# Earlier squares, a shorter look-ahead, later attention constants and a closing norm in fewer steps, in a two-layer encoder trunk

## The chip, the core and the metric

The kernel runs on one core of one Trainium2 chip. The metric is device time in microseconds (us) of one execution. A core has five engines with instruction streams of their own: TensorE (PE in the profile; its weight loads are PEld), VectorE (DVE), ScalarE (ACT), GpSimd (POOL) and SyncE (SP), which here only issues DMA transfers. They wait for one another through semaphores.

## The reference, cut to what matters

256 tokens, width 1024, two layers, all in float32:

```
for l in range(2):
    x = x + 1/2 * SwiGLU_1(RMSNorm(x))        # 1024 -> 2816 gate, up; -> 1024
    h = RMSNorm(x)
    q, k, v (A and B) = h @ w_in[l]
    oA = windowed attention with a sink logit per head
    oB = softmax1 - lambda * softmax2, per-head RMSNorm * (1 - lambda_init)
    x = x + concat(oA, oB) @ w_out[l]
    x = x + 1/2 * SwiGLU_2(RMSNorm(x))
return RMSNorm(x)
# RMSNorm(x) = x / sqrt(mean(x*x) + eps) * g
# SwiGLU(h)  = (silu(h @ w_gate) * (h @ w_up)) @ w_down
# lambda = exp(sum(q1*k1)) - exp(sum(q2*k2)) + lambda_init
```

## The kernel before, in words

**Products.** Every float32 product is made of three products in a faster format (fp32r): an operand is split in a high part, a cast, and a low part, the operand less its high part. PE then adds high x high, low x high and high x low. For weights the cast is ScalarE's and the subtraction VectorE's: `CAST w<-raw` and `TENSOR_TENSOR w<-raw,w` in the profile, 440 of each. Activations are split in the same way (`CAST s<-ps`, then `TENSOR_TENSOR s<-ps,s`).

**Weights.** The program walks through one list of weight steps (`Step`, line 92). A step is a raw tile of 1 MB, of which six can be held (`N_RAW`), and two half-steps, each of which is split into a high and a low tile from a pool of 28 (`s4`). `emit_dma` (147) puts the load on SP's queue, `emit_split` (175) writes the cast and the subtraction into the program. `ahead(n)` (212) writes all splits up to half-step n; `weights()` (233) calls it with twice the step in use plus `look[0]`, and a `Split` calls it again between its halves. So `look[0]` says by how many half-steps the splits stand ahead of PE's products in the program: 8 in an FFN (`IN_FFN`), 6 elsewhere (`IN_MIX`).

**FFN** (`ffn`, 566). The 2816 hidden columns go in five groups of 512 and a piece of 256. Group 0 and 1 are plain: four steps of gate and up weights, `silu` on ScalarE, `hidden` (h = up * silu(gate) on VectorE), then `turn`, which transposes h on PE and splits it, and `down`, the products with w_down. Groups 2, 3 and 4 (`SEVEN`) go through `by_seven` (598): the 2x2 block product with seven products in place of eight. For it, sums of weight blocks are needed: two of a group's raw tiles get a second block added by an accumulating transfer that GpSimd issues (`gather`, 125), and further sums are VectorE's (`plus`, 130, `TENSOR_TENSOR raw<-raw,raw`). Sums of the activations are made once, in group 1 (`make_sums`, 333: the q and v tiles). `down` of a group stands inside the next group. After the last piece, `ffn_end` (704) does the last groups' products: `group(0)`, with `turn` of the last piece in it, and `tail`, the products of the last piece.

**Order.** `Kept` (41) keeps the program's order on each engine, so the order of calls in the source is the order on PE, ScalarE and VectorE. All their instructions carry line 50, that of the helper; they are told apart by their tiles. An engine that waits holds everything behind it.

**The places around the change.** At the start (`take_x`, 410) x arrives in four pieces, is transposed and multiplied by the norm's gain (`pair`, 302), and the first weights are split; then the four squares with their sums (`squares`, 298: ACTIVATE junk<-xk with a read of the accumulator), the norm's factors (`stats`, 368) and small transfers and operations on GpSimd (`constants`, 452). A silu on ScalarE needs the factors, and PE gets no PSUM bank for the next products until the first silu has read one. `attention_constants` (475) makes distances, lambda and gains for the attention: a PE transpose, eleven VectorE operations, an exp on ScalarE. It is handed to the first FFN as `aside` and called in group 1, line 691; the same place in the last FFN calls `final_gain` (974), which loads the final norm's gain (512 KB, on SP). At the end, `close` (993) adds the last products to x and squares the result on ScalarE, and `finish` (1002) reduces the sums on VectorE, takes the power -1/2 on GpSimd, multiplies half the columns on ScalarE and half on VectorE, and issues two outputs on SP.

Of the kernel before, what the change touches and what calls it, by code (L numbers as in the profile page):

```python
# [9 lines left out]
F32 = mybir.dt.float32  # L10
F32R = mybir.dt.float32r
AF = mybir.ActivationFunctionType
ALU = mybir.AluOpType

P = 128
D = 1024
# [7 lines left out]
EPS = 1e-6  # L24
# [5 lines left out]
IN_FFN, IN_MIX = 8, 6  # L30
# [4 lines left out]
def trunk(ctx: ExitStack, tc: tile.TileContext, x, n1, g1, u1, d1, nm, w_in, sink,  # L35
          lq1, lk1, lq2, lk2, subln, w_out, n2, g2, u2, d2, nf, out):
    nc = tc.nc
    sp = nc.sync
# [18 lines left out]
    pe, act, dve, pool = Kept(nc.tensor), Kept(nc.scalar), Kept(nc.vector), Kept(nc.gpsimd)  # L57

    const = ctx.enter_context(tc.tile_pool(name="const", bufs=1))
# [20 lines left out]
    def tmp(tag="tmp", bufs=5, shape=(P, 2, 256), dt=F32):  # L80
        return tp.tile(list(shape), dt, tag=tag, bufs=bufs, name=nm_(tag))
# [127 lines left out]
    look = [IN_MIX]  # L209
# [190 lines left out]
    mhalf = const.tile([P, 8], F32, name="mhalf")  # L400
# [9 lines left out]
    def take_x(k):  # L410

        g, u = early
        if k == 0:
            for j in (0, 1):
                sl = norm.turn(j)
                next(g)
                norm.operands(j, sl)
                next(u)
        elif k == 1:
            for e in (g, u, g, u):  # L420
                next(e)
            norm.pair(2)
            ahead(5)
            norm.pair(3)
        elif k == 2:
            ahead(7)
            for t in range(2):
                for h in range(2):
                    norm.squares(t, h * 512, 512)
            norm.stats()  # L430
            constants()

# [133 lines left out]
    def ffn(norm, aside=None, before=None, final=False):  # L566
        def silu(out_, acc, t):
            act.activation(out_, acc, AF.Silu, scale=norm.r[:, t:t + 1])
            return out_

        def gate(gs):
            g = []
            for t in range(2):
                n = gs[t].shape[1]
                g.append(silu(tmp().rearrange("p a n -> p (a n)")[:, :n], gs[t], t))
            return g

        def up(h, acc, g, t):
            n = acc.shape[1]
            dve.scalar_tensor_tensor(h[:, t, :n], in0=acc, scalar=norm.hr[:, t:t + 1], in1=g, op0=ALU.mult, op1=ALU.mult)  # L580

        def hidden(g, us):
            h = blk(F32)
            for t in range(2):
                up(h, us[t], g[t], t)
            return h

        def prod(xo, w):
            acc = bank()
            for k in range(4):  # L590
                hi, lo = w.part(k)
                xh, xl = xo(k)
                pe.matmul(acc, lhsT=xh, rhs=hi, start=k == 0, stop=False)
                pe.matmul(acc, lhsT=xl, rhs=hi, start=False, stop=False)
                pe.matmul(acc, lhsT=xh, rhs=lo, start=False, stop=k == 3)
            return acc

        def by_seven(h, g):


            flat = lambda: tmp().rearrange("p a n -> p (a n)")

            def put(o, x, y, op):
                dve.tensor_tensor(o, x, y, op=op)
                return o

            m1, m7 = flat(), flat()
            act.copy(m1, prod(norm.quarter(0, 0), weights()))
            act.copy(m7, prod(norm.summed(2), weights(held=True)))
            hT = turn(h, 2)  # L610
            p2 = prod(norm.quarter(0, 1), weights())
            g0 = put(flat(), p2, m1, ALU.add)
            p3 = prod(norm.summed(3), weights())
            silu(g0, g0, 0)
            down(hT, g - 1, 0, weights())
            h = blk(F32)
            p5 = prod(norm.summed(0), weights())
            late = g == max(SEVEN)
            p6 = prod(norm.summed(1), weights(look[0] - 5 if late else 0, late))
            u2 = put(flat(), p6, m1, ALU.subtract)  # L620
            u3 = put(m7, m7, u2, ALU.add)
            p4 = prod(norm.quarter(1, 1), weights(look[0] - 4 if late else 0, late))
            g1 = put(m1, p4, u3, ALU.subtract)
            w = weights(look[0] - 3 if late else 0)
            silu(g1, g1, 1)
            put(u3, u3, p5, ALU.subtract)
            put(u2, u2, p5, ALU.subtract)
            put(u2, u2, p3, ALU.add)
            up(h, u2, g0, 0)
            up(h, u3, g1, 1)  # L630
            down(hT, g - 1, 1, w)
            return h

        def turn(hs, n):
            out_ = []
            for i in range(n):
                sl = halves(bank())
                for c in range(2):
                    for t in range(2):
                        pe.transpose(sl[:, c, t * P:(t + 1) * P], hs[:, t, (2 * i + c) * P:(2 * i + c + 1) * P], ident)  # L640
                hb = blk()
                split(hb, sl)
                out_.append(hb)
            return out_

        accs = [[bank(), bank()] for _ in range(2)]

        def down(hT, g, h, w):
            tokens(accs[h], [None] * (2 * g) + hT, w, 4 * g, last=(FC - 1, G4 - 1) if final and h else FC - 1)


        gs, us = [bank(), bank()], [bank(), bank()]
        if before is None:
            before = norm.late
        look[0] = IN_FFN
        before(0)
        ws = (weights(), weights(2))
        for k in (0, 2):
            if k:
                before(1)  # L660
            for sl, w in zip((gs, us), ws):
                tokens(sl, norm.xs, w, 0, (k, k + 1))
        before(2)
        tokens(gs, norm.xs, weights(), 4)
        g = gate(gs)
        tokens(us, norm.xs, weights(), 4)
        h = hidden(g, us)
        for n in range(1, NGRP):
            sums = norm.make_sums() if n + 1 == min(SEVEN, default=0) else iter(())
            if n in SEVEN:  # L670
                look[0] = IN_FFN - max(0, n - 2)
                h = by_seven(h, n)
                continue
            gs = [bank(), bank()]
            tokens(gs, norm.xs, weights(), 0)
            hT = turn(h, 2)
            norm.copies()
            tokens(gs, norm.xs, weights(), 4)
            g = gate(gs)
            next(sums, None)  # L680
            us = [bank(), bank()]
            for k0 in (0, 4):
                tokens(us, norm.xs, weights(), k0)
                next(sums, None)
            h = hidden(g, us)
            for hh in range(2):
                down(hT, n - 1, hh, weights())
                if hh == 0:
                    next(sums, None)
                    if aside is not None:  # L690
                        aside()
                        aside = None

        gu = [bank(), bank()]
        tokens(gu, norm.xs, weights(), 0)
        hT = turn(h, 2)
        tokens(gu, norm.xs, weights(), 4)
        h = hidden(gate([b[:, 0:256] for b in gu]), [b[:, 256:512] for b in gu])
        return accs, hT, lambda: turn(h, 1)

    BY_TOKENS = [(k, t) for t in range(2) for k in range(2)]
# [266 lines left out]
            res.add(1, t)  # L968
        nxt_norm.late = res.late

    fss = const.tile([P, 2, 4], F32, name="fss")
    gf = []

    def final_gain():
        gf.append(blk(F32))
        sp.dma_start(gf[0].rearrange("p a n -> p (a n)"), nf.partition_broadcast(P))
        pool.memset(fss, 0.0)


    for l in range(DEPTH):  # L980
# [9 lines left out]
            ffn_close(parts, norm)  # L990


    def close(t, c0, n, acc):

        xv = xk[:, t, c0:c0 + n]
        dve.tensor_tensor(xv, acc, xv, op=ALU.add)
        jk = tmp().rearrange("p a n -> p (a n)")
        act.activation(jk[:, :n], xv, AF.Square, accum_out=fss[:, t, c0 // 256:c0 // 256 + 1])
        if c0 == 0:
            pool.tensor_tensor(xv, xv, gf[0][:, 0], op=ALU.mult)  # L1000

    def finish(t):
        rf = tmp("rf", 2, (P, 1))
        dve.tensor_reduce(rf, fss[:, t], axis=mybir.AxisListType.X, op=ALU.add)
        dve.tensor_scalar(rf, rf, 1.0 / D, EPS, op0=ALU.mult, op1=ALU.add)
        pool.tensor_tensor(rf, rf, mhalf[:, 0:1], op=ALU.pow)
        ob = blk(F32)
        act.mul(ob[:, 0], xk[:, t, 0:512], rf)
        dve.scalar_tensor_tensor(ob[:, 1], in0=xk[:, t, 512:D], scalar=rf, in1=gf[0][:, 1], op0=ALU.mult, op1=ALU.mult)
        for j in range(2):  # L1010
            sp.dma_start(out[0, t * P:(t + 1) * P, j * 512:(j + 1) * 512], ob[:, j])

    accs = parts[0]
    group, tail = ffn_end(parts, ((FC - 1), FC - 1))
# [46 lines left out]
```

## Time and profile before

| what | value |
|---|---|
| three timed runs | median 940.94 us (940.77 to 941.16) |
| the profiled execution | 938.1 us, its span 936.3 us |
| mean granted TensorE clock | 0.997 |
| PE busy | 922.1 us, 98% of the span, 4796 matmuls |
| VectorE busy | 757.3 us, 81%, 1066 instructions |
| ScalarE busy | 573.2 us, 61%, 901 instructions |
| GpSimd busy | 51.3 us, 5% |
| chain that ended last | PE 92%, DMA 4%, DVE 1%, ACT 1% |
| mean DMA rate | 208 GB/s, 194.58 MB |

How to read it: times are us from the start of the span. A line of the timeline has a start, a duration (for several instructions in a row, first start to last end), the engine, the line, the operation, output tile <- input tiles, the shapes, and how many; in brackets the idle time ahead of it and what ended it. A line of the waits has the waiting engine and tile, what it waited for, the total in us, how often, and the longest. A line of the windows has, for one stretch, its length and each engine's busy time and count of instructions; PEclk is the granted TensorE clock as a share of full speed. SPq, ACTq and POOLq are an engine's issue of transfers.

### The profile page before, as it was taken

To read this page: it belongs to the slowest core of one execution; us is meant where nothing else is said; L and a number is where in the kernel's file an instruction comes from. 1 tells how busy PE (TensorE), PEld (TensorE's weight loads), DVE (VectorE), ACT (ScalarE), POOL (GpSimd) and SP (SyncE) were. 2 spreads that over 40 slices of the span, in tenths; PEclk is the share of its full clock that TensorE was granted. 3 is DMA by queue.
4 is the path that set the end of the run, shared out by engine and by line. 5 is a ranking of instruction groups with operands and counts; after the bars stand their busy time and mean duration, and the time that the engine had idled before them with its cause. 6 is when DMAs were issued, how large, how long until landed. Compare 5 with 4: busy or idle time off the path is not lost.

```text
span 936.3 us, 12676 instructions
## 1 busy us (share of the span) xinstructions
PE 922.1 (98%) x4796; PEld 782.2 (84%) x4796; DVE 757.3 (81%) x1066; ACT 573.2 (61%) x901; POOL 51.3 (5%) x73
## 2 busy tenths in 40 slices
PE   8999999999999999999999999999999999999997
PEld 6788778899898888888888888888999888888886
DVE  6679999859866588999866799996697566799992
ACT  6847675548745666576475565665577476466562
POOL 0400100000000000100001000000000001001001
PEclk9999999999999999999999999999999999999999
DMA  9986897928425857797667597887462467697821
GB/s 336 355 219 159 247 289 249 270 91 225 136 91 180 249 156 225 206 288 256 240 227 221 135 288 202 240 284 217 150 193 91 135 205 202 166 299 204 249 91 46
DMA packets 110893, 194.58 MB, mean 208 GB/s; under 512 B 3566, under 2 KB 31280, under 8 KB 110832
## 3 DMA queue, kind: packets, MB, share of 16 engines
q1 hardware_dynamic: 96816, 167.27, 53.3%
q0 software_dynamic: 12928, 25.46, 15.4%
q10 hardware_dynamic: 1088, 1.05, 0.3%
q8 instruction: 37, 0.61, 0.3%
q14 instruction: 24, 0.20, 0.1%
HBM read 192.71 MB, written 1.05 MB: 207 GB/s over the span
## 4 chain that ended last, share of the span: by engine, by line
PE 92%; DMA 4%; DVE 1%; ACT 1%; issue 1%; SPq 0%; ACTq 0%; POOLq 0%; POOL 0%; DVEq 0%
PE ps L50 92%; DMA raw<-in_ffn_w_up_dram 2%; DMA raw<-in_ffn_w_gate_dram 2%; DVE w L50 1%; DMA xk<-in_x_dram 1%; ACT w L50 0%; DVE tmp L50 0%; ACT junk L50 0%; DVE s L50 0%; ACT tmp L50 0%; SPq L152 0%; ACT L50 0%; ACTq L50 0%; DVE xk L50 0%; POOLq L1056 0%
## 5 line engine op out<-in xcount | busy, mean ns | idle before, releaser
L50 PE MATMUL ps<-w,s 128*128 128x512 f32 (+1 forms) x2754 | 642.1, 391 | 2.1 <-ACT tmp L50 2.1
L50 PEld LDWEIGHTS ps<-w,s 128*128 128x128 f32 x2754 | 512.7, 189 | 107.8 <-ACT tmp L50 2.6
L50 DVE TENSOR_TENSOR w<-raw,w 128x1024 fp32r<-128x1024 f32 (+1 forms) x440 | 460.8, 1093 | 57.0 <-ACT w L50 55.8
L50 ACT CAST w<-raw 128x1024 fp32r<-128x1024 f32 (+1 forms) x440 | 391.1, 948 | 85.8 <-DVE raw L50 71.0
L50 PE MATMUL ps<-w,q 128*128 128x512 f32 x432 | 101.9, 389 | 0.0
L50 PEld LDWEIGHTS ps<-w,q 128*128 128x128 f32 x432 | 81.1, 188 | 16.8
L50 PE MATMUL ps<-s,w 128*128 128x256 f32 x672 | 84.1, 285 | 0.0
L50 PEld LDWEIGHTS ps<-s,w 128*128 128x128 f32 x672 | 81.7, 192 | 1.1
L50 ACT ACTIVATE s<-ps,gcol 128x256 fp32r<-128x256 f32 (+1 forms) x80 | 31.5, 488 | 48.0 <-PE ps L50 48.0
L50 ACT CAST s<-ps 128x512 fp32r<-128x512 f32 x48 | 26.1, 593 | 51.9 <-PE ps L50 51.9
L50 DVE TENSOR_TENSOR raw<-raw,raw 128x1024 f32<-128x1024 f32 x48 | 56.4, 1216 | 0.0
L50 DVE TENSOR_TENSOR s<-ps,s 128x512 fp32r<-128x512 f32 x48 | 31.0, 684 | 27.1 <-ACT s L50 27.1
L50 POOL DMA_DIRECT2D raw<-in_ffn_w_up_dram x24 | 31.0, 1293 | 354.9 <-DVE w L50 163.2
L50 PE MATMUL ps<-ident,s 128*128 128x128 f32 x304 | 40.2, 274 | 1.4 <-DVE s L50 1.3
L50 PEld LDWEIGHTS ps<-ident,s 128*128 128x128 f32 x304 | 35.0, 141 | 7.2 <-DVE s L50 2.8
L50 ACT ACTIVATE tmp<-tmp,r 128x512 f32<-128x512 f32 x24 | 17.3, 722 | 35.5 <-DVE tmp L50 35.5
L50 ACT ACTIVATE s<-s,negm 128x256 f32<-128x256 f32 x64 | 31.9, 500 | 5.4 <-DVE negm L50 5.2
L50 PE MATMUL ps<-w,v 128*128 128x512 f32 x144 | 34.6, 389 | 0.0
L50 ACT CAST q<-tmp 128x512 fp32r<-128x512 f32 x20 | 12.4, 620 | 35.0 <-DVE tmp L50 34.9
L50 PEld LDWEIGHTS ps<-w,v 128*128 128x128 f32 x144 | 27.0, 188 | 5.6
L50 DVE SCALAR_TENSOR_TENSOR s<-ps,gcol,s 128x256 fp32r<-128x256 f32 x48 | 20.3, 478 | 12.3 <-ACT s L50 12.3
L50 DVE TENSOR_TENSOR xk<-xk,ps 128x512 f32<-128x512 f32 (+1 forms) x25 | 14.2, 598 | 17.6 <-PE ps L50 17.6
(107 smaller groups left out, 426.1 us busy)
## 6 DMA issues: line engine op xcount, KB each, us to landing
raw<-in_ffn_w_down_dram SPq DMA_DIRECT2D x44, 1024.0 KB, 6.0
raw<-in_ffn_w_gate_dram SPq DMA_DIRECT2D x39, 1024.0 KB, 5.9
raw<-in_ffn_w_up_dram SPq DMA_DIRECT2D x39, 1024.0 KB, 5.6
raw<-in_ffn_w_up_dram POOLq DMA_DIRECT2D x24, 1024.0 KB, 11.2
raw<-in_w_in_dram SPq DMA_DIRECT2D x14, 1024.0 KB, 5.5
raw<-in_ffn_w_gate_dram SPq DMA_DIRECT2D x8, 512.0 KB, 6.4
raw<-in_ffn_w_up_dram SPq DMA_DIRECT2D x8, 512.0 KB, 7.4
raw<-in_w_in_dram SPq DMA_DIRECT2D x8, 512.0 KB, 6.8
```

What stands on the lines that cost most here:

```text
L50: ins = issue(*a, **k)
```

## The change

Four edits:

1. In `take_x` the four squares go from behind the last of the first casts to places between them: one ahead of pair 2, one behind it, one behind pair 3, one where all were.
2. In the first FFN of the first layer (`before is take_x`) `look[0]` is 6 in groups 2, 3 and 4; it was 8, 7 and 6. The other FFNs keep 8, 7 and 6.
3. `aside` is called at the end of the FFN, behind the last `hidden`, and no longer in group 1: this moves the attention constants in the first FFN and the load of the final gain in the last one.
4. The closing norm: the square and sum of each piece is one VectorE instruction, which starts from the sum of the piece before (the first from D * EPS), so that the reduce and the scaling in `finish` fall away; the factor sqrt(D) that this leaves out is multiplied into the final gain on GpSimd beforehand, in place of the clearing of the old sums. Of the two outputs of `finish` one is issued by ScalarE and one by SP.

```diff
@@ take_x
             for e in (g, u, g, u):
                 next(e)
+            norm.squares(0, 0, 512)
             norm.pair(2)
+            norm.squares(1, 0, 512)
             ahead(5)
             norm.pair(3)
+            norm.squares(0, 512, 512)
         elif k == 2:
             ahead(7)
-            for t in range(2):
-                for h in range(2):
-                    norm.squares(t, h * 512, 512)
+            norm.squares(1, 512, 512)
             norm.stats()
             constants()
@@ ffn
             if n in SEVEN:
-                look[0] = IN_FFN - max(0, n - 2)
+                look[0] = IN_FFN - max(0, n - 2) if before is not take_x else IN_MIX
                 h = by_seven(h, n)
                 continue
...
                 if hh == 0:
                     next(sums, None)
-                    if aside is not None:
-                        aside()
-                        aside = None
...
         h = hidden(gate([b[:, 0:256] for b in gu]), [b[:, 256:512] for b in gu])
+        if aside is not None:
+            aside()
         return accs, hT, lambda: turn(h, 1)
@@ final_gain
-    fss = const.tile([P, 2, 4], F32, name="fss")
...
-        pool.memset(fss, 0.0)
+        pool.tensor_scalar(gf[0], gf[0], math.sqrt(D), 0.0, op0=ALU.mult, op1=ALU.add)
@@ close, finish
+    tot = [tmp("tot", 4, (P, 1)) for _ in range(2)]
+    for t in range(2):
+        dve.memset(tot[t], D * EPS)
...
-        act.activation(jk[:, :n], xv, AF.Square, accum_out=fss[:, t, c0 // 256:c0 // 256 + 1])
+        s_ = tmp("tot", 4, (P, 1))
+        dve.tensor_tensor_reduce(out=jk[:, :n], in0=xv, in1=xv, scale=1.0, scalar=tot[t], op0=ALU.mult, op1=ALU.add,
+                                 accum_out=s_)
+        tot[t] = s_
...
         rf = tmp("rf", 2, (P, 1))
-        dve.tensor_reduce(rf, fss[:, t], axis=mybir.AxisListType.X, op=ALU.add)
-        dve.tensor_scalar(rf, rf, 1.0 / D, EPS, op0=ALU.mult, op1=ALU.add)
-        pool.tensor_tensor(rf, rf, mhalf[:, 0:1], op=ALU.pow)
+        pool.tensor_tensor(rf, tot[t], mhalf[:, 0:1], op=ALU.pow)
...
-        for j in range(2):
-            sp.dma_start(out[0, t * P:(t + 1) * P, j * 512:(j + 1) * 512], ob[:, j])
+        for j, q in enumerate((act, sp)):
+            q.dma_start(out[0, t * P:(t + 1) * P, j * 512:(j + 1) * 512], ob[:, j])
```

## The prediction

> **What bounds the kernel now.** The page first: TensorE is busy for nearly the whole span, so only three things can shorten it: a PE stall, a stretch at half clock, or the ends.
>
> ```profile
> PE 922.1 (98%) x4796; PEld 782.2 (84%) x4796; DVE 757.3 (81%) x1066; ACT 573.2 (61%) x901; POOL 51.3 (5%) x73
> ```
>
> Next the waits of PE in the first 141 us, and busy time by windows (columns: PE, PEld, DVE, ACT, POOL, PEclk, DMA share, GB/s).
>
> ```profile
> PE ps L50 <- DMA grow<-in_ffn_norm_dram: 3.4, 1, 3.4
> PE ps L50 <- ACT tmp L50: 2.1, 1, 2.1
> PE ps L50 <- DVE s L50: 1.3, 3, 0.7
> ```
>
> ```profile
> 30.90:33.04 2.14, 0.00 (x1) 0.00 (x0) 1.95 (x2) 2.11 (x4) 2.14 (x5) 1.00 1.05 387
> 33.27:36.69 3.42, 3.42 (x9) 2.64 (x9) 2.16 (x2) 3.42 (x5) 2.97 (x16) 0.50 1.06 376
> 57.87:181.44 123.57, 122.12 (x553) 100.29 (x552) 117.81 (x131) 78.79 (x92) 5.10 (x4) 1.00 0.81 236
> ...
> 138.50:929.80 791.30, 791.25 (x4225) 675.96 (x4223) 643.37 (x926) 479.49 (x772) 33.36 (x29) 1.00 0.66 198
> ```
>
> See four things. (1) PE does nothing from 30.90 to 33.04, and from 33.27 to 36.69 it runs at half clock: 3.42 us that do 1.71 us of work, so 1.71 are lost. (2) PE also waits for VectorE near 105 and 137; counted with the slow restart behind each, these two stalls take 1.36 (104.85 to 106.55) and 0.84 (137.09 to 138.27). (3) From 138.5 to 929.8 there is no stall: whatever shift PE has at 140 or at the end of the first FFN goes through to the end unchanged. (4) From 57.87 to 181.44 VectorE is itself busy 117.81 of 123.57 us. It is the second bound, right behind PE.
>
> **The first stall.** The ScalarE timeline (start, duration):
>
> ```profile
> 28.38 0.63 ACT L50 ACTIVATE junk<-xk 128x512 f32<-128x512 f32 x1
> ...
> 29.01 1.98 ACT L50 CAST w<-raw 128x1024 fp32r<-128x1024 f32 x2
> 31.01 1.28 ACT L50 ACT_TABLE_LOAD   x1
> 32.30 1.27 ACT L50 ACTIVATE tmp<-ps,r 128x512 f32<-128x512 f32 x2
> ```
>
> All eight PSUM banks are held, so PE waits for the first silu. Ahead of it stand four squares (26.12 to 29.1), two casts and the table load. In the changed order one square with its read (0.63 + 0.18) goes into the idle 13.03 to 14.14, the second into 14.98 to 16.09; the third delays the casts behind it by 0.75, inside the waits for DMA of 0.43 and 0.71 that follow; the fourth stays, 26.12 to 26.9. The data of the casts lands at 26.86, so: casts 26.9 to 28.9, table to 30.2, first silu (0.69) to 30.9. PE's last matmul is issued at 30.51; its stall shrinks from 2.14 to about 0.2, and with it I expect the half clock to go, since it begins in the slice right behind the stall. PE then runs **up to 2.0 + 1.7 = 3.7 to 3.8 earlier** (I take 3.8).
>
> **The split weights and the constants.** PE is early, but VectorE may not follow. Its stretch starts at 57.87 because of ScalarE's cast at 56.79, which waited for a transfer that GpSimd issued at 43.21 and which landed at 56.69:
>
> ```profile
> 56.79 2.00 ACT L50 CAST w<-raw 128x1024 fp32r<-128x1024 f32 x2 [2.75 <-DMA raw<-in_ffn_w_up_dram]
> ```
>
> Nothing in the change moves that issue. From there to the last operand of the first FFN, VectorE has the same instructions before and after, in another order: a look-ahead of 6 half-steps in place of 8, 7, 6 takes splits (1.14 each in a row) from in front of the sums that make a group's h, and the constants (11 operations, 67.70 to 71.26, with 0.27 of waiting 3.3 of work) go from the end of group 1 to the end of the FFN, in front of the last splits. The first effect should remove the stall of group 2:
>
> ```profile
> 105.08 1.41 DVE L50 SCALAR_TENSOR_TENSOR s<-tmp,hr,tmp 128x512 f32<-128x512 f32 x2
> ```
>
> Two splits fewer ahead of it are 2.3 us against 1.36. But what is put off piles up at the next turn and at the end of the FFN, which is here:
>
> ```profile
> 176.08 0.87 DVE L50 SCALAR_TENSOR_TENSOR s<-ps,hr,tmp 128x256 f32<-128x256 f32 x2
> 177.05 2.36 DVE L50 TENSOR_TENSOR w<-raw,w 128x1024 fp32r<-128x1024 f32 x2
> ...
> 180.13 0.59 ACT L50 CAST s<-ps 128x512 fp32r<-128x512 f32 x1 [2.16 <-PE ps L50]
> ...
> 180.75 0.69 DVE L50 TENSOR_TENSOR s<-ps,s 128x512 fp32r<-128x512 f32 x1 [1.33 <-ACT s L50]
> ```
>
> After the change the constants stand between the first and the second line. The split at 180.75 ends at 181.44; PE uses it at 182.93. VectorE's new end is 57.87 + 117.81 + its idle time. Idle before was 5.76: 1.4 for the q and v sums (their cast on ScalarE comes between, stays), 0.3 lex (stays), 2.3 waits for casts of w (mostly raw tiles that a GpSimd transfer completes; I keep 2.1), 1.33 at the last line (I keep 0.9, since VectorE comes there later), 0.4 small. Together about 5.1, so the end is at 180.8, and PE's **shift here is 180.8 - 182.93 = -2.1**. Bounds: with 3.7 of idle -3.5, with 6.3 -0.9. PE alone could be earlier by 3.8 + 1.36 + 0.84 = 6.0; so some 3.9 us come back as waits for VectorE, at the turns of groups 3 and 4 (about 1.5 to 2) and before the last tail of this FFN (about 2).
>
> ScalarE has two table loads fewer (8 to 6; 1.28 each): it is busy 78.79 of that stretch, so they are worth nothing on the path, or at most what they take from a cast that VectorE waits for (0 to 0.3). PE's extra transpose of the constants only changes place. Without VectorE's bound, the constants at the FFN's end would cost 3.3 less the room there (1.33 idle and 1.49 until PE's use, 2.8, less some issue gaps): 0.5 to 0.9.
>
> **The last gain and the tail.** The load of the final gain (512 KB) goes to SP's end, behind every weight load; it waits there for a tile that PE reads until about 906 and then lands by 912 (the page's issue rows take 5.5 to 7.4), plus a GpSimd multiply of 128x1024, at most twice the 1.29 of GpSimd's 128x512 operations. It is needed at 922.9: 8 us of cover; nothing stands behind it on SP but the outputs.
>
> ```profile
> 930.31 0.42 ACT L50 ACTIVATE tmp<-xk 128x256 f32<-128x256 f32 x1 [0.49 <-DVE xk L50]
> ...
> 930.85 0.16 DVE L50 TENSOR_REDUCE rf<-fss 128x1 f32<-128x4 f32 x1 [0.63 <-ACT tmp L50]
> 931.04 0.15 DVE L50 TENSOR_SCALAR rf<-rf 128x1 f32<-128x1 f32 x1
> 931.27 0.56 POOL L50 TENSOR_TENSOR rf<-rf,mhalf 128x1 f32<-128x1 f32 x1 [3.18 <-DVE rf L50]
> ```
>
> PE's last matmul ends at 929.75, the add at 930.21, the power starts at 931.27. After: a multiply-and-reduce of 128x256 on VectorE behind the add (0.42 to 0.48, from VectorE's custom rows with an accumulator in the attention), a read of 0.08, and the hand to GpSimd (0.08 after the ts above): the power starts near 930.76, so 0.5 less. SP issues the two halves at 932.61 and 933.04; from two queues the second goes 0.43 earlier. Bounds: 0 to 0.5 for each. **Tail: -0.9.**
>
> **Sum.** -2.1 - 0.9 = -3.0. The profiled execution took 938.1 (its span 936.3), so 935.1; the runs shown have a median of 940.94, 2.8 above it, and the same step there gives **937.9**. A measurement of this kernel can tell about 0.2%, 1.9 us.
>
> **Rivals.**
> R1, the forecast: VectorE's end sets the shift. For it: 117.81 of 123.57. Own range -1.4 to -4.4 (bounds of idle and tail): 936.5 to 939.5. Chance 0.47.
> R2, VectorE does not hold PE: idle shrinks further, and all stalls go. -6.0 + 0.9 (constants) - 0.9 = -6.0: 934.9. Against it: idle would have to fall to about 2. Chance 0.15.
> R3, one of the returned stalls, about 2 us at the end of the FFN, is followed by half clock as the one at 30.90 was: 3.42 at 0.50 loses 1.7. -3.0 + 1.7 = -1.3: 939.6. For it: the 2.14 us stall had this behind it; against it: the 1.36 stall at 105 had not, and the slices of 3.41 us in which the clock is decided must fall badly. Chance 0.20. The Trainium skill, "TensorE: Matmul & The Clock Gate", section "HAM oscillation — how this bites in real kernels", says that only PE gaps of more than about 3.4 us should be feared. By that rule a 2 us stall would leave the clock alone and R3 falls; the row at 33.27 speaks against it, since 2.14 us of idle were enough there.
> R4, slower: the shorter look-ahead delays the accumulating transfers. GpSimd issues the second one of a group only when VectorE has split the raw tile it adds to; with 8 to 6 half-steps in group 2 and 7 to 6 in group 3 that split comes two and one half-steps later. A half-step is 6 matmuls of 0.22 us (30 us hold 136), 1.3 us: 2.6 + 1.3 = 3.9 of lateness, and these transfers take 10.7 to 13.5 from issue to landing and were waited for already (2.75 at 56.79). With one half-clock stretch, 3.9 + 1.7 = 5.6: -3.0 + 5.6 = +2.6, 943.5. It decides once lateness and clock exceed 3.0 + 1.9 = 4.9. Against it: in the trace most raw tiles of groups 2 to 4 land with some us in hand. Chance 0.13.
> R5, the change doesn't do what it says: the squares wait for x or delay the first casts as much as they save, the stall at 30.90 stays near 2, and the constants cost 0.9 at the end of the FFN: +0.9 - 0.9, with up to 0.4 more, 941.3. Chance 0.05.
>
> **Numbers.** R2, R1 and R3 hold 0.82, so the range goes from 934.6 to 940.4. Faster by over 0.2% (below 939.06): R1 and R2 less 0.02, 0.60. Within: R3, R5 and 0.02, 0.27. Slower (above 942.82): R4, 0.13.
>
> **What will show it.** In the changed profile: PEclk 1.00 in 33 to 37 and first silu near 30.2; the stall near 105 (now near 101) gone; waits of PE for VectorE's or ScalarE's s near 101, 134 and 179 to 181; VectorE's last split of the FFN ending near 180.8; 6 table loads; the power about 0.5 nearer to PE's end and outputs on two queues. I am wrong if the half clock stays, if VectorE idles more than 7 us from 57.87 to that split, or if a wait shows up between 185 and 929.

## The result and the profile after

| | before | changed |
|---|---|---|
| median of 4 runs each | 940.86 us | 935.46 us (935.0 to 936.25) |
| ratio | | 0.9943, 95% interval 0.9926 to 0.996 |
| the profiled execution | 938.1, span 936.3 | 935.0, span 933.2 |
| mean granted clock | 0.997 | 0.999 |

The change is faster by 5.4 us. The profiled executions differ by 3.1 only; why they do is a finding of its own, below. A second set of runs beside the experiments gave 0.995 (0.9937 to 0.9964).

The page of the changed kernel, first part: the same work of PE on a shorter span.

```profile
PE 921.1 (99%) x4796; PEld 780.7 (84%) x4796; DVE 759.9 (81%) x1074; ACT 566.8 (61%) x889; POOL 55.0 (6%) x73
```

The start, on ScalarE: the squares stand between the casts, the first silu starts at 29.65 (it was 32.30), and PE has no wait there.

```profile
25.52 0.62 ACT L50 ACTIVATE junk<-xk 128x512 f32<-128x512 f32 x1
...
26.34 2.00 ACT L50 CAST w<-raw 128x1024 fp32r<-128x1024 f32 x2
28.36 1.28 ACT L50 ACT_TABLE_LOAD   x1
29.65 1.27 ACT L50 ACTIVATE tmp<-ps,r 128x512 f32<-128x512 f32 x2
```

The busy time by windows (columns as in the prediction): the clock is 1.00 where it was 0.50, and VectorE's stretch, from its own start to the split that ends it, is 120.49 long with 117.53 busy.

```profile
33.27:36.69 3.42, 3.42 (x18) 2.82 (x18) 3.42 (x5) 1.43 (x2) 2.52 (x17) 1.00 1.11 278
59.21:179.70 120.49, 118.78 (x536) 96.84 (x534) 117.53 (x132) 78.06 (x92) 5.13 (x4) 1.00 0.82 243
```

The waits of PE from 25 to 932: three, all for VectorE, 1.7 in all, of which 1.1 at the end of the first FFN. The timeline there shows the splits that stand behind the constants (whose last operation ends at 176.33); PE goes on at 179.75.

```profile
PE ps L50 <- DVE s L50: 1.7, 3, 1.1
```

```profile
176.73 2.36 DVE L50 TENSOR_TENSOR w<-raw,w 128x1024 fp32r<-128x1024 f32 x2 [0.40 <-ACT w L50]
177.56 0.57 ACT L50 CAST s<-ps 128x512 fp32r<-128x512 f32 x1
...
179.01 0.68 DVE L50 TENSOR_TENSOR s<-ps,s 128x512 fp32r<-128x512 f32 x1
...
179.75 1.43 PE L50 MATMUL ps<-w,s 128*128 128x512 f32 x5 [1.07 <-DVE s L50]
```

The end: one add, one multiply-and-reduce, a read, the power.

```profile
926.92 0.42 DVE L50 TENSOR_TENSOR xk<-ps,xk 128x256 f32<-128x256 f32 x1 [0.53 <-PE ps L50]
927.38 0.48 DVE L50 CUSTOM_DVE_ANT_0 tmp<-xk,tot 128x256 f32<-128x256 f32 x1
927.79 0.08 DVE L50 DVE_READ_ACCUMULATOR2_ANT tot<- 128x1 f32 x1
927.95 0.56 POOL L50 TENSOR_TENSOR rf<-tot,mhalf 128x1 f32<-128x1 f32 x1 [3.21 <-DVE tot L50]
```

From PE's last matmul (926.88 in the trace, 929.75 before) to the power it is 1.07 us, before 1.52; from there to the end of the span it is 5.28, before 5.06.

### The profile page after: what moved, and what is told of

Read it like the earlier page. It is cut to its first block, busy times and chain, and to the rows that moved or that the text cites. A ratio compares the mean times of both kernels' runs of the same rounds, so it can differ in the third digit from the quotient of the medians.

```text
span 933.2 us, 12665 instructions
## 1 busy us (share of the span) xinstructions
PE 921.1 (99%) x4796; PEld 780.7 (84%) x4796; DVE 759.9 (81%) x1074; ACT 566.8 (61%) x889; POOL 55.0 (6%) x73
## 4 chain that ended last, share of the span: by engine, by line
PE 93%; DVE 4%; issue 1%; DMA 0%; ACT 0%; POOLq 0%; POOL 0%; ACTq 0%; DVEq 0%
PE ps L50 93%; DVE w L50 3%; DVE s L50 1%; DMA xk<-in_x_dram 0%; DVE tmp L50 0%; DVE raw L50 0%; ACT w L50 0%; DVE distA L50 0%; DVE xk L50 0%; DVE distB L50 0%; POOLq L1060 0%; POOL rf L50 0%; ACTq L50 0%; DVE lsum L50 0%; DVEq L50 0%
## 5 line engine op out<-in xcount | busy, mean ns | idle before, releaser
L50 ACT COPY tmp<-ps 128x512 f32<-128x512 f32 x24 | 14.0, 584 | 22.6 <-PE ps L50 22.5
```

The lines of the kernel that those rows point to most:

```text
L50: ins = issue(*a, **k)
```

## The experiments

The theories that the expectations name. V, the forecast: VectorE's total of work up to the first FFN's end sets the shift. C: half-clock stretches that follow the start stall make the difference. P was formed after the first four runs: a pin, ScalarE's queue from group 2's first accumulating transfer to the copy that frees a PSUM bank.

### The kernel before, once more

No edit.

> The kernel before, unchanged. Its profiled execution took 938.1, its timed runs 940.66 to 941.16: 2.8 apart. Theory C (clock): most executions lose one or more half-clock stretches (1.7 each) beyond the one seen at 33.27, so a second profile shows 940 to 941 with PEclk below 1.00 in another slice, and spans and clocks of the runs move together. Theory V (VectorE alone): the profiled execution is typical in its stalls, and the 2.8 lie outside the PE stream (start, end, or something not in the span). Ratio to itself 1.000 within 0.001 under both.

Measured: 940.9 against 940.29, ratio 1.0007 (0.9998 to 1.0015). The second profile has a span of 938.3 and looks different from the first. PE's waits from 40 to 930:

```profile
PE ps L50 <- ACT tmp L50: 3.2, 1, 3.2
PE ps L50 <- DVE s L50: 0.7, 2, 0.3
```

The start stall is 0.6 here and no half clock follows it. Instead PE waits 3.2 at 73, behind the turn of group 1, and the half clock comes there:

```profile
72.15 1.03 PE L50 MATMUL ps<-ident,s 128*128 128x128 f32 x8
76.40 2.07 PE L50 MATMUL ps<-w,s 128*128 128x512 f32 x4 [3.21 <-ACT tmp L50]
```

```profile
76.04:79.45 3.41, 3.05 (x7) 2.48 (x8) 3.41 (x5) 3.41 (x6) 0.00 (x0) 0.50 0.20 26
```

ScalarE's timeline says what it waits for: a copy at 75.77 that reads a PSUM bank, and in front of it a queue that begins with a cast at 58.17.

```profile
58.17 2.00 ACT L50 CAST w<-raw 128x1024 fp32r<-128x1024 f32 x2 [6.15 <-PE ps L50]
...
67.82 0.62 ACT L50 CAST v<-tmp 128x512 fp32r<-128x512 f32 x1 [3.05 <-DVE tmp L50]
68.46 1.28 ACT L50 ACT_TABLE_LOAD   x1
71.88 0.20 ACT L50 ACTIVATE lex<-lsum 128x4 f32<-128x4 f32 x1 [2.14 <-DVE lsum L50]
71.99 3.87 ACT L50 CAST w<-raw 128x1024 fp32r<-128x1024 f32 x4
75.77 0.58 ACT L50 COPY tmp<-ps 128x512 f32<-128x512 f32 x1
```

The releaser in brackets at 58.17 is not the cause (PE had long been done): the raw tile's accumulating transfer lands at 58.07 in the trace. In the first profile it landed at 56.69, and the same copy and PE met there:

```profile
74.40 0.57 ACT L50 COPY tmp<-ps 128x512 f32<-128x512 f32 x1
```

```profile
74.14 1.03 PE L50 MATMUL ps<-ident,s 128*128 128x128 f32 x8
75.02 3.01 PE L50 MATMUL ps<-w,s 128*128 128x512 f32 x12
```

The copy ended at 74.97, PE went on at 75.02. No wait is listed, but two chains ended within 0.05 us of each other. And the first profile was not typical: 59 further executions of the kernel before, run beside these experiments, have spans of 936.6 to 940.1 with a median of 938.5, all longer than its 936.3. C is right that the half clock moves its place. Its other sign, spans and clocks that move together, is not seen: the longest execution of this set (span 940.9) has the highest clock, 0.999. V is right that a part lies outside the span (941.17 less 938.3 is 2.9 in this execution, 938.1 less 936.3 was 1.8 in the first); that the first profile is typical in its stalls fails. The start stall is 2.1 and 0.6 in the two profiles of this kernel.

### The squares alone

```diff
 before.py
+            norm.squares(0, 0, 512)
             norm.pair(2)
... (edit 1 of the change, nothing else)
```

> Only the squares are moved. Theory V: PE arrives 3.8 earlier at group 2, but VectorE's order is the old one, so the stalls at the turns of groups 2 and 3 grow to about 3 and 2, and the time falls by only 0.5 to 2. Theory C: a large part of the 5.4 is half clock that follows the start stall, so the time falls by 3.5 to 5.5, nearly all of the change's gain.

Measured: 940.64, ratio 1.0003 (0.9995 to 1.0012). Both theories miss. The start stall is gone (no wait near 31), and PE gives all of it back at 71:

```profile
PE ps L50 <- ACT tmp L50: 5.1, 1, 5.1
```

```profile
73.52:80.35 6.83, 4.10 (x10) 3.23 (x11) 6.83 (x8) 6.03 (x9) 0.00 (x0) 0.50 0.24 63
```

The cast is at 58.03, the copy at 75.62: unmoved. A stall ahead of this pin is free, and here a longer wait even costs a second slice of half clock.

### The change without the squares

```diff
 after.py
-            norm.squares(0, 0, 512)
... (the four squares behind ahead(7) again)
```

> The changed kernel with the squares in their old place. Theory V: the start stall and its half clock stay (3.8 at PE), but VectorE was late by 1.3 to 2 at the first FFN's end in the changed kernel and hides as much of it: slower than the changed kernel by 2 to 3, 2.5 to 3.5 faster than before. Theory C: slower than the changed kernel by 4 to 5.5, about as before.

Measured: 935.89 (934.73 to 937.83), ratio 0.9958 (0.9944 to 0.9972): within the noise of the changed kernel, 4.4 faster than before. PE waits 1.0 at 31 here, with no half clock behind it, and 1.1 at 178; the changed kernel has the second wait alone. V's mechanism is right that VectorE hides the start: PE goes on at 72.10 behind the turn of group 1, 1.28 later than in the changed kernel, and at 179.94 behind the wait at 178, only 0.19 later, as VectorE's stretch starts 0.20 later (59.41 against 59.21). V's 2 to 3 is too much; C falls.

### The look-ahead of before, and the constants of before

```diff
 after.py (e5)
-                look[0] = IN_FFN - max(0, n - 2) if before is not take_x else IN_MIX
+                look[0] = IN_FFN - max(0, n - 2)
 after.py (e6)
+                    if aside is not None:
+                        aside()
+                        aside = None
... (in group 1 again, and no longer at the FFN's end)
```

> The changed kernel with the look-ahead of 8, 7 and 6 half-steps. Theory V: splits stand in front of the sums again; PE, earlier by 3.8, waits at the turn of group 2 for VectorE by 3 or more: 1 to 3 slower than the changed kernel, with a half-clock stretch behind the stall when it exceeds 2. Rival (the look-ahead only shifts waits between places, VectorE's total being the same): within 0.5 of the changed kernel.

> The changed kernel with the attention constants (and the load of the final gain) back in group 1. Theory P (a pin): in every run so far the cast behind group 2's first accumulating transfer starts near 58.1, whatever PE did before; from there ScalarE's queue leads to the copy that frees a PSUM bank for PE: 17.6 us later in the kernel before (75.77), 12.1 in the changed one (70.20). The exp, its table load and its wait for lsum are 3.4 of the difference, two casts 1.9. With the constants back the copy comes near 73.7, PE waits about 3 us behind the turn of group 1, with half clock behind it: 2 to 4.5 slower than the changed kernel, 1 to 3 faster than before. Theory V (VectorE's total work to the first FFN's end): the constants are done either way, so within 0.8 of the changed kernel.

Measured: 937.27 (ratio 0.9973, 0.9964 to 0.9983) and 937.67 (0.9973, 0.9964 to 0.9981). With one half of the pair alone the kernel is 2.5 to 3 us faster than before, with both 4.7 to 5.4. The copy tells why, counted from the cast behind the transfer (start of cast, start of copy, difference):

| kernel | cast | copy | us | PE's wait there |
|---|---|---|---|---|
| before, again | 58.17 | 75.77 | 17.6 | 3.2 |
| constants in group 1, look-ahead 6 | 58.37 | 74.08 | 15.7 | 3.5 |
| constants at the end, look-ahead 8, 7, 6 | 58.16 | 72.12 | 14.0 | 1.7 |
| changed | 58.13 | 70.20 | 12.1 | none |

A look-ahead of 6 takes two casts (1.9) out of this queue, the constants' move takes the table load and the wait for lsum (3.6). For the constants P's numbers, on record before the run, hold, and V's (within 0.8) fails. For the look-ahead P came after the result; there V's 1 to 3 slower came true, but not at its place: PE waits 1.7 for ScalarE's copy, and its longest wait for VectorE at the turn of group 2 is 0.7, where 3 or more was expected. PE's wait does not follow the copy alone; it is longer the earlier PE arrives. The wait for the sum of lambda is where VectorE's eleven operations reach PE: through ScalarE's queue, not through VectorE's own splits.

In the changed kernel copy and PE still meet:

```profile
70.20 0.57 ACT L50 COPY tmp<-ps 128x512 f32<-128x512 f32 x1
```

```profile
70.82 3.01 PE L50 MATMUL ps<-w,s 128*128 128x512 f32 x12
```

The copy ends at 70.77. PE goes on 1.00 behind the start of its transposes (69.82), and 0.79 behind it in the kernel without the squares (71.31 to 72.10), where the copy is done 1.1 earlier. So the pin still holds PE here, by about 0.2.

### Only the exp later

```diff
 before.py, attention_constants
-        lex = const.tile([P, 2, DEPTH], F32, name="lex")
-        act.activation(lex, lsum, AF.Exp)
-        dve.tensor_tensor(nlam, lex[:, 1], lex[:, 0], op=ALU.subtract)
... (these and the two adds to nlam at the end of the first FFN)
```

> The kernel before, with only the exp of lambda and the three small operations behind it at the end of the first FFN; the other constants stay in group 1. Theory P: ScalarE loses the table load and the wait for lsum ahead of the casts, the copy moves from 75.8 to about 72.4, PE's wait there falls from 3.2 to below 0.5 and no half clock follows: 2 to 4.5 faster than before. Theory V: VectorE keeps all but 0.5 us of its work in the old order, so at most 0.7 faster than before.

Measured: 939.13, ratio 0.9991 (0.9981 to 1.0): 1.2 faster, between the two expectations. The pin goes as P said: copy at 72.71, no listed wait of PE at 73, no half clock (the only slow slice is behind the last product). But PE, early now, waits for VectorE in groups 2 and 3 (waits from 90 to 200):

```profile
PE ps L50 <- DVE s L50: 1.8, 4, 0.7
PE ps L50 <- DVE tmp L50: 1.7, 2, 1.0
```

So V is the next bound behind P: with the old look-ahead VectorE's splits stand in front of the sums. The two waits add up to 3.5, where the second profile of before has 0.7; that this is why the time falls short of P's is read from one profile.

### Without the first accumulating transfer

```diff
 before.py, seven
-                Step(4, 512, load(b), key=b, behind=gather(c, b), prep=gather(b, a)),
+                Step(4, 512, load(b), key=b, behind=gather(c, b) if len(specs) > 15 else None, prep=gather(b, a)),
```

> The kernel before, without the first accumulating transfer of group 2 of the first FFN (one block is left out of one sum of weights). Theory P: the cast that waited for it no longer does; it starts 4 us or more earlier, the copy behind the constants too, PE's wait of 3.2 near 73 falls below 0.5: 2.5 to 5 faster than before. Theory V: VectorE's stretch starts earlier by as much, and the waits at the turns shrink too, so also faster, but the wait at 73 would not need to go first. Against both: if the next accumulating transfer (landing near 64) holds the casts in its place, at most 1 faster.

Measured: 933.83, ratio 0.9933 (0.9921 to 0.9946), 6.6 faster than before; one block is left out of one sum. The cast starts at 51.80, the copy at 69.55, and PE goes on at 72.81 without a wait, although the constants and the look-ahead are those of before and the start stall is there (1.7). The landing of this one transfer is what pins the kernel before. The gain is more than P's 2.5 to 5; the wait and its half clock (3.2 + 1.7) do not cover it, and the rest was not followed up.

### The constants later still

```diff
 after.py
-        parts = ffn(norm, attention_constants, take_x) if l == 0 else ffn(norm)
+        parts = ffn(norm, None, take_x) if l == 0 else ffn(norm)
-        ffn_close(parts, norm_m)
+        ffn_close(parts, norm_m, attention_constants if l == 0 else None)
... (ffn_close hands it to ffn_end, which calls it behind its last weights())
```

> The changed kernel with the constants still later, behind the last splits of the first FFN (and the final gain's load likewise as in the changed kernel, at the FFN's end). In the changed kernel PE waits 1.1 for VectorE's s at 178.2 to 179.75. Theory P and V alike: this wait goes, as the constants stand in front of that split; 0.8 to 1.5 faster than the changed kernel, unless the 3.4 us of constants delay the residual's sums behind them, where PE has no wait so far: then 0 to 2 slower.

Measured: 934.16 (933.21 to 934.63), ratio 0.9934 (0.9922 to 0.9947). PE has no wait from 141 to 932: the 1.1 at 178 is gone, and the residual's sums do not suffer. Against the changed kernel's ratios, 0.9943 and 0.995, from other sets of runs, it is 0.8 to 1.5 us faster, as expected; the intervals overlap.

### Four kernels on one chip

The changed kernel again; the last one with both outputs on SP; the last one with two loads of w_down on GpSimd's queue behind the two accumulating transfers; the change with the old closing norm.

```diff
 e11: constants later still
-        for j, q in enumerate((act, sp)):
+        for j, q in enumerate((sp, sp)):
 e12: constants later still
+LATE = (14, 18)
-                sp.dma_start(dst, src)
+                (pool if i in LATE else sp).dma_start(dst, src)
 e3: after.py with close, finish and final_gain's GpSimd line of before.py
```

> The changed kernel again, beside the next three on one chip. All theories: 4 to 6 faster than before; cast behind group 2's first accumulating transfer near 58, no wait of PE above 0.3 at the turn of group 1, one of 1.0 to 1.4 near 178.

> The kernel with the constants behind the last splits, both outputs of the closing norm on SP. Forecast of record (the second issue on another queue gains up to 0.43): 0.4 slower at the end than with two queues, in the profile the last landing 3.3 behind the first issue. Rival from the changed kernel's profile (both outputs share the DMA engines and land together 2.86 behind the issue, against 2.68 for the second of two issues in a row): 0.1 to 0.2 faster at the end. The whole stays within 1 of the kernel with the constants behind the last splits, 4.5 to 7.5 faster than before.

> The kernel with the constants behind the last splits, and two loads of w_down (used in group 2) issued by GpSimd behind group 2's two accumulating transfers, where SP issued them at 38 and 44 to 46. Theory P, with the pin set by the share of the DMA engines: loads land one every 2.7 us until 63, so two loads fewer in front let the first accumulating transfer land 2 to 4.5 earlier (53.5 to 56), the cast starts then, the waits left at 71 and 132 shrink: 0.5 to 2 faster than the kernel with the constants behind the last splits. Rival: the accumulating transfer needs its 10.5 us and more whatever shares the engines; it lands no more than 1 earlier and the time stays within 0.4.

> The changed kernel with the old closing norm. Forecast of record: 0.9 slower than the changed kernel. From the changed kernel's profile: the power starts 0.46 earlier behind PE's end, the outputs take 0.17 to 0.22 longer: 0.25 slower than the changed kernel, which the timed runs can hardly tell; in the profile 6.5 to 6.6 from PE's last matmul to the end of the span, against 6.3.

| kernel | median (range of 5) | ratio to before | PE end to power | power to span end |
|---|---|---|---|---|
| changed | 935.21 (935.11 to 935.84) | 0.995 (0.9937 to 0.9964) | 1.06 | 5.29 |
| e3, old closing norm | 935.54 (934.78 to 936.27) | 0.9954 (0.9942 to 0.9967) | 1.52 | 5.05 |
| e11, both on SP | 933.65 (932.9 to 934.87) | 0.9935 (0.9922 to 0.9947) | 1.06 | 5.06 |
| e12, loads behind | 933.43 (933.21 to 933.82) | 0.9932 (0.9919 to 0.9944) | 1.07 | 5.98 |

The closing norm: the shorter chain saves 0.46 and the second queue loses 0.2. In the changed kernel both outputs are issued at 929.29 and 929.32 and land within 0.2 of each other, the later one 2.84 behind the first issue; in the kernels with one queue the second is issued 0.42 later and lands 2.68 behind the first issue. The rival of that expectation holds, the forecast of record does not. In e12 one output took 3.4 to land; a spread of this size is in the ends of single runs (in the kernel with only the exp later the last one, on one queue, lands 3.60 behind the first issue).

The loads: in e12 the transfer is issued at 44.03 and lands at 53.63, 9.6 us later; in the changed kernel it takes 14.4 (43.64 to 58.03). The DMA engines are busy throughout in both (share 1.04 and 1.08). ScalarE starts the cast at 53.73, and PE has no wait at all from 25 to the end of its work.

```profile
53.73 2.00 ACT L51 CAST w<-raw 128x1024 fp32r<-128x1024 f32 x2 [2.68 <-DMA raw<-in_ffn_w_up_dram]
```

So what sets the pin is the share of the DMA engines: from 43 to 49 loads of 1 MB land one every 2.7 us or so, and in the kernels with all loads on SP two of w_down, not needed before group 2's products, run beside the transfer. The landing came as forecast (53.5 to 56), the time did not: in place of 0.5 to 2 faster, e12 has a ratio of 0.9932 against 0.9934 of the kernel with the constants behind the last splits, and is 0.2 below e11, whose outputs go by one queue, the way that ends 0.2 sooner. In time the rival's "within 0.4" holds. Both beat the changed kernel on the same chip (no run of e12 or e11 reaches its fastest, 935.11); e12, 1.8 us below it, has the lowest median here of the kernels that compute everything, but e11 is within noise of it.

## Why the prediction was right in sign and short in size

It said 937.9, 3.0 less; measured 5.4 and, again, 4.7 less. The profiled execution came out at 935.0 against the 935.1 worked out for it, but that is luck: its starting point was 2.2 us below the median span of 59 executions. The measured 935.46 lies outside R1's own range (936.5 to 939.5), nearer to R2's 934.9. Still R1's mechanism is what the changed kernel shows at the end of the first FFN: VectorE's split ends at 179.70 and PE goes on at 179.75. What the prediction lacked is the bound of the kernel before. Step by step:

- **The first stall**: the step itself came true (silu 0.6 earlier than worked out, half clock gone). Its 3.8 stands in no term of the sum, since 3.9 of PE's 6.0 were to come back as waits, and it came back whole: alone the squares bring 0, and the change without them is as fast within noise. What stood behind it in the kernel before was a pin that does not move with PE.
- **VectorE's stretch starts at the landing of the accumulating transfer, and nothing moves that**: right in kind. In size the prediction took one execution's 56.69 where the other eleven profiles with this transfer and all loads on SP show 57.5 to 59.0 (VectorE's start is 59.21 in the changed kernel).
- **The table load and the exp "worth nothing on the path, or 0 to 0.3"**: this is the term that failed. They stood in the queue between that landing and the copy that gives PE its bank, and cost 3.6 with the wait for lsum; the two casts that the shorter look-ahead moves cost 1.9 there. The first profile had the copy's end and PE's start at 74.97 and 75.02. The prediction looked at waits and at the operands' producers, and there is neither in a tie on a bank that comes free. The Trainium skill, "ScalarE: Activation LUTs", section "What ACT_TABLE_LOAD costs", puts a switch of tables at about 2.66 us, the load and a drain. Here the load takes 1.28, the cast in front of it ends 0.02 earlier and silu follows within 0.01 (28.36 to 29.65), so the measurement decides. What cost more behind the load of the exp was the wait for VectorE's sum, 2.14.
- **VectorE's idle time, 5.1**: measured 3.0 over the changed stretch (120.49 less 117.53); the wait of 1.33 at the last split is gone, and of the 2.3 for casts about 0.7 is left; why the latter went was not looked into. The start came 1.3 later than reckoned and the idle time was 2.1 less, and the two partly cancel: 59.21 + 117.53 + 2.96 is 179.70, where 180.8 was forecast. PE's shift between the first profiles is 3.2 there (182.93 to 179.75) and 2.9 at its last matmul, where 2.1 was forecast.
- **Waits given back**: they came at 132 and 178, not at 101, and are 1.7 in all where 3.9 was forecast. The sign of being wrong that it named, a wait between 185 and 929, shows in the changed kernel's second profile alone: 0.3 at 594.
- **R3**, half clock behind a returned wait: did not come, since the longest wait is 1.1. It was the right rival in the wrong kernel: 55 of the 59 executions of the kernel before have a mean granted clock of 0.997 or less, as its two profiles with one slice of half clock, and all nine of the changed kernel 0.998 or more. At which place the slice lies, only the two profiles show.
- **R4**, late transfers through the shorter look-ahead: no sign; group 2's second transfer is issued earlier than before (49.16 against 53.08 and 51.08).
- **The tail**: -0.9 forecast, -0.23 measured. The chain's 0.5 was right (0.46), the second queue's 0.43 has the wrong sign. The final gain had its cover, although GpSimd's multiply took 2.90, more than twice the 1.29: it started at 904.36, and the gain is first used at 920.18.

In the typical profile of before (the second one) PE's last matmul ends at 931.72, in the changed kernel's first profile at 926.88: 4.8 earlier. The wait at 73 and its half clock, 3.2 + 1.7, come to as much; all other waits of PE differ by 0.6 in sum (6.3 and 5.7). With the 0.2 of the tail that is the 5.1 between the spans, 938.3 and 933.2.

## What to carry to other kernels

Two chains that meet within a tenth of a microsecond do not show as a wait; look, at each place where PE takes a buffer that another engine frees, at when that engine was done, and at a second execution before pricing anything behind it. Time won ahead of a point that a transfer pins was worth nothing here; find the pin first (the same start in every variant gives it away), then count every instruction in the queue of the engine between it and the bound engine, a table load and a wait for another engine's small result included. When the transfers of a stage fill the DMA engines, the order of the loads is part of the schedule.

## What the runs showed of the hardware

- Half clock behind a PE wait: none behind waits of 1.1 and 1.7 us, one slice of 3.41 behind 2.1 and 3.2, two slices (6.83) behind 3.5 and 5.1. The Trainium skill, "TensorE: Matmul & The Clock Gate", section "HAM oscillation — how this bites in real kernels", fears only gaps of more than about 3.4; here 2.1 was enough, so the measurement decides.
- A GpSimd-issued accumulating transfer of 1 MB took 9.6 us when the two loads of w_down were issued behind it and the next one (at 50.86 and 51.63, with the transfer from 44.03 to 53.63), and 13.5 to 14.6 in the twelve profiles in which SP had issued them at 38 to 48.
- Two outputs of 256 KB issued at once on two queues landed within 0.2 of each other, the later one 2.84 behind the issue; issued 0.42 apart on one queue, the second landed 2.68 behind the first issue. Single profiles of either kind lie 0.6 to 0.9 above.
